# Shift and scale of four channel tiles as product and sum along a channel's weights on VectorE, the other tiles in pairs, and x normalized in front

## The chip, the cores and the metric

The kernel runs on one core of one Trainium2 chip. The metric is the device time in microseconds of one execution. A core has five engines with an instruction stream each: TensorE (PE, whose weight loads are listed as PEld), VectorE (DVE), ScalarE (ACT), GpSimd (POOL) and SyncE (SP, which here issues the loads). Each engine works through its own stream in order, and semaphores hold an instruction until its data or its buffer is ready.

## What is computed

One layer of a hybrid backbone over 256 latent tokens and 256 context tokens, with d = 2048 channels, all in float32. The stage that the change touches computes the modulated, normalized input and the first columns of its projection:

```
sc = jax.nn.silu(c)
scc = jax.nn.silu(c_ctx)
shift, scale, gate = jnp.split(sc @ w_ada[l] + b_ada[l], 3, axis=-1)
shift_c, scale_c, gate_c = jnp.split(scc @ w_ada[l] + b_ada[l], 3, axis=-1)
hc = _rmsnorm(ctx, g_pre[l]) * (1.0 + scale_c) + shift_c
zc = hc @ w_in[l][:, :XBC_W + DT_W]
...
hx = _rmsnorm(x, g_pre[l]) * (1.0 + scale[:, None]) + shift[:, None]
zx = hx @ w_in[l]
```

Behind it stand a convolution and silu, a bidirectional state-space scan over both streams, a gated MLP group over the latent tokens, and the output projection. The change leaves all of that as it is.

## The kernel before

**Layout.** Channels lie on the 128 partitions, in 16 tiles (kt = 0 to 15); xT holds both streams, 512 tokens to a tile (context in columns 0 to 255, latent in 256 to 511). Every float32 product runs as three matmuls, on a rounded part and a rest of each factor: hhi and hlo are the two parts of the modulated input, hi_st and lo_st those of the weights. The helper mm3 (L138 to L140) issues the three.

**The first stage.** SP loads xT in four transfers of 1 MB, then wada (shift and scale weights, 32 transfers of 1 MB, two for each channel tile) and wst (the first 960 columns of the input projection, a transfer of 0.48 MB for each tile). The squares of x (L264 on DVE for odd tiles, L266 on ACT for even ones) are summed on PE into pss, and a few small steps turn that into rb, 1/rms for every token on all partitions. While that runs, `warm` (L256) issues matmuls on ones, whose result nobody reads.

**Shift and scale.** `ada_mm(ci)` multiplies chunk ci of wada, one transfer, with silu(c) and silu(c_ctx) on PE into psada (L215). The tiles come in units: tile 0, tile 1, then pairs; a pair has four chunks. `ada_fin(u)` transposes psada into adat on DVE (L222), and ACT makes ha = g (1 + scale) and hb = shift from it, two small activations for each tile (L224, L226).

**The modulated input.** `make_h(kt)` multiplies a tile of xT by ha and rb (two DVE instructions for the two streams, L307), adds hb and rounds to hhi (two ACT instructions, L310), and takes the rest to hlo (two on DVE, L312). `split_st(kt)` splits wst: a cast on ACT (L299) and two differences on DVE (L300, L301).

**The products of the stage.** For each tile PE adds two matmuls to psdt (L362, L363) and three each to seven column blocks psx0 to psx6. In the order of a row these are the steps ("m", -1) for psdt and ("m", 0) to ("m", 6). The function `row_steps(kt)` lists what stands in row kt: m (those steps), a (`ada_mm`), f (`ada_fin`), h (`make_h`) and s (`split_st`) of the next tile. In the last row `z` copies two finished psx to the segments zq (L357), and `dt_tok` copies psdt and brings its columns to tokens with eight matmul passes pstok (L320) against the matrix fold, which a reduce on DVE (L165) has made from the identity at the start.

**What sets the order.** PE, DVE, ACT and POOL are under a manual schedule: instructions stand in the order in which the code issues them. SP's loads stand in the order of the code too, and each waits for its buffer: six raw buffers for wada, three for wst.

Of the kernel before, what the change touches and what calls it, by code (L numbers as in the profile page):

```python
# [41 lines left out]
def tile_hybrid_ssd_mlp(  # L42
# [121 lines left out]
    A = yseg(7)[:, 320:384]  # L164
    nc.vector.tensor_reduce(fold, ident.rearrange("p (g m) -> p m g", g=2), axis=mybir.AxisListType.X, op=ALU.add)  # L165
# [12 lines left out]
    sc2 = stp.tile([P, KT, 2], F32, name="sc2")  # L178
    nc.sync.dma_start(sc2, ccols)
# [9 lines left out]

    def ada_place(ci):  # L190

        if ci < 4:
            return ci // 2, 64, 8 * (ci % 2), 8
        return ci // 4 + 1, 128, 4 * (ci % 4), 4

    def ada_load(*cs):
# [8 lines left out]
    def ada_mm(ci):  # L205
        u, n, k0, nk = ada_place(ci)
        if k0 == 0:
            ada_ps[u] = spt([P, 512], f"psada{u}")
        ps = ada_ps[u]
        raw = ada_raw.pop(ci)  # L210
        for kk in range(nk):
            k = k0 + kk
            for g in range(4):
                o = (kk * 4 + g) * n
                nc.tensor.matmul(ps[32 * g : 32 * g + 32, 0:n], lhsT=sc[:, k, :], rhs=raw[:, o : o + n],  # L215
                                 start=k == 0, stop=k == KT - 1)

    def ada_fin(u):
# [3 lines left out]
        nc.vector.transpose(tr[:, 0:n], ps[:, 0:n])  # L222
        for q, kt in enumerate(UNITS[u]):
            nc.scalar.activation(ha[:, kt, :], tr[:, 64 * q : 64 * q + 2], AF.Identity, bias=bsc1[:, kt : kt + 1],  # L224
                                 scale=pc[:, C_GPRE + kt : C_GPRE + kt + 1])
            nc.scalar.activation(hb[:, kt, :], tr[:, 64 * q + 32 : 64 * q + 34], AF.Identity,  # L226
                                 bias=pc[:, C_BADA + kt : C_BADA + kt + 1])
# [33 lines left out]
    for k in range(KT):
        sq = yseg((1, 2, 3, 6, 0)[k % 5])
        if k % 2:
            nc.vector.tensor_tensor(sq, xT[:, k, :], xT[:, k, :], op=ALU.mult)  # L264
# [3 lines left out]
        nc.tensor.matmul(pss[32 * g : 32 * g + 32, :], lhsT=ones[:, 0:32], rhs=sq, start=k < 4, stop=k >= KT - 4)
# [26 lines left out]
    def split_st(kt):  # L295
        raw = wraw[kt]
        hi = wp["spl"].tile([P, WST + 64], F32R, tag="hi", name=f"hi_st{kt}")
        lo = wp["spl"].tile([P, WST - 64], F32R, tag="lo", name=f"lo_st{kt}")
        nc.scalar.copy(hi[:, 64:], raw)  # L299
        nc.vector.tensor_tensor(hi[:, 0:64], raw[:, 0:64], hi[:, 64:P].bitcast(F32), op=ALU.subtract)  # L300
        nc.vector.tensor_tensor(lo, raw[:, 64:], hi[:, P:].bitcast(F32), op=ALU.subtract)  # L301
        return hi, lo

    def make_h(kt):
        sl = (slice(256, 512), slice(0, 256))
        for v, s in enumerate(sl):
            nc.vector.scalar_tensor_tensor(xT[:, kt, s], xT[:, kt, s], ha[:, kt, v : v + 1], rb[:, s],  # L307
                                           op0=ALU.mult, op1=ALU.mult)
        for v, s in enumerate(sl):
            nc.scalar.activation(hhi[kt][:, s], xT[:, kt, s], AF.Identity, bias=hb[:, kt, v : v + 1])  # L310
        for v, s in enumerate(sl):
            nc.vector.scalar_tensor_tensor(hlo[kt][:, s], xT[:, kt, s], hb[:, kt, v : v + 1],  # L312
                                           hhi[kt][:, s].bitcast(F32), op0=ALU.add, op1=ALU.subtract)


    def dt_tok():
        nc.scalar.copy(zdt, psdt)
        ps = spt([P, 4, 64], "pstok")
        for t in range(4):
            nc.tensor.matmul(ps[:, slot[t], :], lhsT=zdt[:, t * P : (t + 1) * P], rhs=fold, start=True, stop=True)  # L320
        nc.vector.tensor_tensor(zt.rearrange("p (t h) -> p t h", t=4), ps, bc(dtc, 1, 4), op=ALU.add)
# [3 lines left out]
    def row_steps(kt):  # L325


        m = [("m", i) for i in range(-1, NST)]
# [16 lines left out]
        return nxt[1:] + a + f + nxt[:1] + m

    def step(kt, what, i):
        if what == "a":
# [5 lines left out]
        elif what == "s":  # L354
            sp0[i] = split_st(i)
# [13 lines left out]
    sp0[0] = split_st(0)  # L369
    ada_fin(0)  # L370
    make_h(0)
    for kt in range(KT):
# [848 lines left out]
```

## Time and profile before

| | us |
|---|---|
| three runs | 998.97, 999.53, 1000.25 |
| median | 999.53 |
| the profiled execution, its own time | 999.99 |
| its span in the trace | 998.3 |
| first psdt matmul (tile 0) starts | 23.21 |
| last tile's psdt matmul starts | 128.63 |
| first matmul of the next stage starts | 134.16 |

Times within the span count from its start. "Tile" in the rows that follow is a channel tile. The page gives busy time for each engine; a window gives the same for a stretch of the span; the chain follows back from the last instruction to what released it; the groups sum instructions of one line and shape and say what ended the idle time ahead of them (behind the second bar, after the arrow); the timeline lists instructions with start, duration and, in brackets, the idle time ahead with its releaser. In the rows of a single source line the three numbers behind the colon are the shortest, median and longest duration in ns, and "x64" behind a matmul counts passes, of which a float32 matmul whose parts aren't rounded has several.

### The profile page before, as it was taken

The numbers are of one execution on the slowest core, as the hardware profiler recorded it, in microseconds if no ns is written. First come the engines' busy times: TensorE is split into PE (matmuls) and PEld (weight loads), VectorE is DVE, ScalarE is ACT, GpSimd is POOL, SyncE is SP. The second block draws the span as 40 slices with busy tenths as digits, with TensorE's granted clock in tenths as the row PEclk, the third lists the DMA queues.
The fourth block names the chain that finished last, engine by engine and source line by source line (L and its number), as shares of the span: only waits on it lengthen the run. The fifth ranks groups of instructions, "written<-read, shape, count | busy, mean of one in ns | idle before, by whom it ended". The sixth has DMA issues, their size and how long they took to land.

```text
span 998.3 us, 14183 instructions
## 1 busy us (share of the span) xinstructions
PE 977.1 (98%) x5636; PEld 791.3 (79%) x5636; DVE 629.9 (63%) x944; ACT 493.0 (49%) x759; POOL 113.7 (11%) x162
## 2 busy tenths in 40 slices
PE   7999999999999999999999999999999999999996
PEld 3788888778687878787888888877888888888885
DVE  4344478877977665666667766666565564445636
ACT  4233347666656545544445343455565564346522
POOL 0000003423443222224000000000000000000000
PEclk9999999999999999999999999999999999999998
DMA  9999744333224323235878778674555545556722
GB/s 380 419 417 419 293 175 143 111 127 127 85 85 165 103 112 133 79 127 195 311 283 297 275 258 319 252 274 172 185 173 191 188 169 209 175 207 231 274 85 84
DMA packets 31554, 207.28 MB, mean 208 GB/s; under 512 B 4080, under 2 KB 4208, under 8 KB 7808
## 3 DMA queue, kind: packets, MB, share of 16 engines
q1 hardware_dynamic: 28656, 192.52, 51.5%
q0 software_dynamic: 2112, 12.65, 3.6%
q10 hardware_dynamic: 720, 1.20, 0.3%
q8 instruction: 44, 0.72, 0.3%
q14 instruction: 22, 0.18, 0.1%
HBM read 204.20 MB, written 2.16 MB: 207 GB/s over the span
## 4 chain that ended last, share of the span: by engine, by line
PE 69%; issue 11%; DMA 9%; DVE 8%; POOL 1%; ACT 1%; SPq 0%; DVEq 0%; POOLq 0%; ACTq 0%
PE psx L138 9%; PE psx L140 9%; PE psx L139 9%; PE pa L1026 5%; PE pa L1028 5%; PE pa L1027 5%; DMA gate<-in_wada_dram 5%; PE pm L1073 3%; PE pm L1075 3%; PE pm L1074 3%; PE psada L215 3%; DVE xbc L495 2%; PE pq L1075 2%; PE pq L1073 2%; PE pq L1074 2%
## 5 line engine op out<-in xcount | busy, mean ns | idle before, releaser
L82 DVE TENSOR_TENSOR lo_w<-w,hi_w 128x1024 fp32r<-128x1024 f32 x173 | 210.5, 1224 | 144.3 <-ACT hi_w L81 144.3
L81 ACT CAST hi_w<-w 128x1024 fp32r<-128x1024 f32 x173 | 182.1, 1053 | 202.5 <-PE pa L1028 130.5
L1026 PE MATMUL pa<-hi_w,hhi 128*128 128x512 f32 x512 | 202.5, 395 | 0.0
L1028 PE MATMUL pa<-hi_w,hlo 128*128 128x512 f32 x512 | 199.5, 390 | 0.0
L1027 PE MATMUL pa<-lo_w,hhi 128*128 128x512 f32 x512 | 199.4, 389 | 0.0
L138 PE MATMUL psx<-hhi,hi_w 128*128 128x512 f32 (+1 forms) x400 | 153.5, 384 | 1.3 <-DVE xbc L495 1.3
L140 PE MATMUL psx<-hhi,lo_w 128*128 128x512 f32 (+1 forms) x400 | 146.0, 365 | 0.0
L139 PE MATMUL psx<-hlo,hi_w 128*128 128x512 f32 (+1 forms) x400 | 145.7, 364 | 0.0
L1026 PEld LDWEIGHTS pa<-hi_w,hhi 128*128 128x128 f32 x512 | 96.2, 188 | 20.7 <-issue 1.6
L1028 PEld LDWEIGHTS pa<-hi_w,hlo 128*128 128x128 f32 x512 | 96.1, 188 | 20.2
L1027 PEld LDWEIGHTS pa<-lo_w,hhi 128*128 128x128 f32 x512 | 96.2, 188 | 19.4 <-issue 0.2
L495 DVE SCALAR_TENSOR_TENSOR xbc<-psx,pc,xbc 128x248 f32<-128x248 f32 (+1 forms) x204 | 83.6, 473 | 36.6 <-ACT xbc L479 35.6
L420 DVE TENSOR_TENSOR lo_w<-w,hi_w 128x1024 fp32r<-128x1024 f32 x61 | 78.1, 1287 | 25.0 <-ACT hi_w L414 25.0
L138 PEld LDWEIGHTS psx<-hhi,hi_w 128*128 128x128 f32 x400 | 75.5, 189 | 15.0 <-issue 3.1
L140 PEld LDWEIGHTS psx<-hhi,lo_w 128*128 128x128 f32 x400 | 75.4, 189 | 12.6
L139 PEld LDWEIGHTS psx<-hlo,hi_w 128*128 128x128 f32 x400 | 75.6, 189 | 12.1 <-issue 1.7
L414 ACT CAST hi_w<-w 128x1024 fp32r<-128x1024 f32 x61 | 63.4, 1044 | 26.4 <-PE pa L1028 13.3
L884 DVE SCALAR_TENSOR_TENSOR junk<-gate,cb 128x2048 bf16<-128x2048 f32 x16 | 36.6, 2290 | 24.6 <-DMA gate<-in_wada_dram 24.6
L1073 PE MATMUL pm<-hi_w,hhi 128*128 128x512 f32 x128 | 50.0, 390 | 0.0
L1074 PE MATMUL pm<-lo_w,hhi 128*128 128x512 f32 x128 | 49.9, 390 | 0.0
L1075 PE MATMUL pm<-hi_w,hlo 128*128 128x512 f32 x128 | 49.7, 389 | 0.0
L138 PE MATMUL psx<-hhi,hi_st 128*128 128x512 f32 (+1 forms) x112 | 41.3, 369 | 0.0
(219 smaller groups left out, 1333.7 us busy)
## 6 DMA issues: line engine op xcount, KB each, us to landing
w<-in_wlat_dram SPq DMA_DIRECT2D x64, 1024.0 KB, 4.8
ada<-in_wada_dram SPq DMA_DIRECT2D x32, 1024.0 KB, 14.6
w<-in_wout_dram SPq DMA_DIRECT2D x32, 1024.0 KB, 4.8
w<-in_wxbc_dram SPq DMA_DIRECT2D x25, 1024.0 KB, 4.8
gate<-in_wada_dram SPq DMA_DIRECT2D x16, 1024.0 KB, 5.7
R<-acs POOLq DMA_DIRECT2D x8, 1024.0 KB, 4.9
wst<-in_wst_dram SPq DMA_DIRECT2D x16, 480.0 KB, 14.8
xT<-in_xch_dram SPq DMA_DIRECT2D x4, 1024.0 KB, 8.0
```

The lines of the kernel that those rows point to most:

```text
L81: nc.scalar.copy(hi, raw)
L82: nc.vector.tensor_tensor(lo, raw, hi.bitcast(F32), op=ALU.subtract)
L138: nc.tensor.matmul(ps, lhsT=whi, rhs=hhi[k][:, s], start=start, stop=False)
L139: nc.tensor.matmul(ps, lhsT=whi, rhs=hlo[k][:, s], start=False, stop=False)
L140: nc.tensor.matmul(ps, lhsT=wlo, rhs=hhi[k][:, s], start=False, stop=stop)
L495: nc.vector.scalar_tensor_tensor(ao, zi, cw[:, k : k + 1], ao, op0=ALU.mult, op1=ALU.add)
L1026: nc.tensor.matmul(pa[tk], lhsT=hhi[k][:, t], rhs=whi[:, w], start=k == 0, stop=False)
L1027: nc.tensor.matmul(pa[tk], lhsT=hhi[k][:, t], rhs=wlo[:, w], start=False, stop=False)
L1028: nc.tensor.matmul(pa[tk], lhsT=hlo[k][:, t], rhs=whi[:, w], start=False, stop=k == KT - 1)
L1073: nc.tensor.matmul(p, lhsT=yh[:, t], rhs=whi[:, w], start=j == 0, stop=False)
L1074: nc.tensor.matmul(p, lhsT=yh[:, t], rhs=wlo[:, w], start=False, stop=False)
L1075: nc.tensor.matmul(p, lhsT=yl[:, t], rhs=whi[:, w], start=False, stop=hf == 0 and j == 15)
```

## The change

Four of the 16 channel tiles, 7, 10, 13 and 15 (VTILES), get shift and scale on DVE. Their weights lie transposed in wada, one channel on each partition, and `ada_v` multiplies the 2048 weights of a channel with silu(c) and sums along them in one instruction (four for a tile: scale and shift, each with c and with c_ctx). For that silu(c) and silu(c_ctx) must stand on all partitions; `c_rows` makes them in the first stage with eight diagonals on DVE and eight matmuls against ones (psr), and `c_keep` copies them to y on ACT. They stand where `warm(1)` stood in the loop over the squares. The other tiles form the units (0), (1), (2,3), (4,5), (6,8), (9,11), (12,14).

A table of strings, WITH, now sets each row's order: `p4` is four of the row's own steps m, `a4.1` a chunk of unit 4, `f`, `h` and `s` as before, `v10.0.1` one sum of tile 10 (0 for scale, 1 for c_ctx), `e10` its ha and hb, `n` the normalizing of tiles 4 to 15. A string LOADS sets the order of the transfers, `room` and `give` issue each as soon as a buffer is free. There are five raw buffers at first, as the sixth holds the squares (sq4), and six from rb on. The bytes moved are the same.

1/rms is multiplied into xT in front (`norm`, one DVE instruction for each tile). `make_h` then has no products on DVE: ACT forms x ha + hb, for tiles 0 to 3 straight into hhi (and DVE a second time in full precision), from tile 4 on into xT itself, followed by a cast into hhi; hlo is one DVE instruction over 512 columns. The split of wst runs two tiles ahead. The reduce for fold moves into `dt_tok`, as y's segments hold the rows of silu(c) until then; A gets a buffer of its own.

```diff
+UNITS = ((0,), (1,), (2, 3), (4, 5), (6, 8), (9, 11), (12, 14))
+VTILES = (7, 10, 13, 15)
+LOADS = "u0.0 w0 u0.1 u1.0 u1.1 w1 w2 u2.0 u2.1 u2.2 u2.3 w3 w4 v7.0 u3.0 u3.1 u3.2 u3.3 w5 v7.1 w6 u4.0 u4.1 u4.2 u4.3 " \
+        "w7 w8 w9 v10.0 v10.1 u5.0 u5.1 u5.2 u5.3 w10 w11 w12 v13.0 v13.1 u6.0 u6.1 u6.2 u6.3 w13 w14 v15.0 w15 v15.1"
+WITH = (
+    "p2 a1.0 a1.1 f1 h1 n p4 a2.0 p2 a2.1",
+    "p2 a2.2 p2 a2.3 f2 h2 h3 s3 p4",
+    "s4 v7.0.0 v7.0.1 p6 a3.0 p2 a3.1",
+    "p2 a3.2 p2 a3.3 f3 h4 s5 h5 p4",
+    "v7.1.0 s6 v7.1.1 e7 h7 p6 a4.0 p2 a4.1",
+    "p2 a4.2 p2 a4.3 f4 h6 s7 h8 p4",
+    "s8 v10.0.0 p8",
+    "s9 v10.0.1 v10.1.0 p4 a5.0 p2 a5.1 p2 a5.2",
+    "v10.1.1 e10 h10 p3 a5.3 f5 h9 s10 h11 p5",
+    "s11 v13.0.0 p8",
+    "s12 v13.0.1 v13.1.0 p3 a6.0 p2 a6.1 p2 a6.2 p1",
+    "v13.1.1 e13 h13 p1 a6.3 f6 h12 s13 h14 p7",
+    "s14 v15.0.0 v15.0.1 p8",
+    "s15 v15.1.0 v15.1.1 e15 h15 p8",
+    "p8",
+    "",
+)
...
+    def ada_v(kt, c, v):
+        raw = ada_raw[f"v{kt}.{c}"]
+        nc.vector.scalar_tensor_tensor(junk, raw, 1.0, y[:, v, :], op0=ALU.mult, op1=ALU.mult,
+                                       accum_out=vsum[:, kt, c, v : v + 1])
...
+    def c_rows(*bs):
+        for b in bs:
+            v, k = b // 4, 4 * (b % 4)
+            dg = junk4[:, (b % 2) * 512 : (b % 2 + 1) * 512].rearrange("p (k m) -> p k m", k=4)
+            nc.vector.tensor_tensor(dg, bc(ident, 1, 4), bc(sc[:, k : k + 4, v], 2, P), op=ALU.mult)
+            cbp[b] = acp.tile([P, 512], F32, tag="acc", name=f"psr{b}")
+            nc.tensor.matmul(cbp[b], lhsT=ones, rhs=dg, start=True, stop=True)
+
+    def c_keep(*bs):
+        for b in bs:
+            nc.scalar.copy(y[:, b // 4, (b % 4) * 512 : (b % 4 + 1) * 512], cbp.pop(b))
...
     warm(2)
+    c_rows(0, 1)
...
         if g == 3:
-            warm(1)
+            b = k // 4 * 2
+            c_keep(b, b + 1)
+            if b < 6:
+                c_rows(b + 2, b + 3)
...
+    def norm(*ks):
+        for k in ks:
+            nc.vector.tensor_tensor(xT[:, k, :], xT[:, k, :], rb, op=ALU.mult)
...
     def make_h(kt):
...
-        for v, s in enumerate(sl):
-            nc.vector.scalar_tensor_tensor(xT[:, kt, s], xT[:, kt, s], ha[:, kt, v : v + 1], rb[:, s],
-                                           op0=ALU.mult, op1=ALU.mult)
-        for v, s in enumerate(sl):
-            nc.scalar.activation(hhi[kt][:, s], xT[:, kt, s], AF.Identity, bias=hb[:, kt, v : v + 1])
-        for v, s in enumerate(sl):
-            nc.vector.scalar_tensor_tensor(hlo[kt][:, s], xT[:, kt, s], hb[:, kt, v : v + 1],
-                                           hhi[kt][:, s].bitcast(F32), op0=ALU.add, op1=ALU.subtract)
+        x = xT[:, kt, :]
+        if kt < 4:
+            for v, s in enumerate(sl):
+                nc.scalar.activation(hhi[kt][:, s], x[:, s], AF.Identity, bias=hb[:, kt, v : v + 1],
+                                     scale=ha[:, kt, v : v + 1])
+            full = ss4
+            for v, s in enumerate(sl):
+                nc.vector.tensor_scalar(full[:, s], x[:, s], ha[:, kt, v : v + 1], hb[:, kt, v : v + 1],
+                                        op0=ALU.mult, op1=ALU.add)
+        else:
+            full = x
+            for v, s in enumerate(sl):
+                nc.scalar.activation(x[:, s], x[:, s], AF.Identity, bias=hb[:, kt, v : v + 1], scale=ha[:, kt, v : v + 1])
+            nc.scalar.copy(hhi[kt], x)
+        nc.vector.tensor_tensor(hlo[kt], full, hhi[kt].bitcast(F32), op=ALU.subtract)
...
     def dt_tok():
+        nc.vector.tensor_reduce(fold, ident.rearrange("p (g m) -> p m g", g=2), axis=mybir.AxisListType.X, op=ALU.add)
         nc.scalar.copy(zdt, psdt)
```

Where the order of instructions matters below, here it is at three places. Names carry the number of a buffer behind the last underscore, "x2" is two alike in a row.

PE before, at the end of the loop over the squares (psw is a filler matmul, psb the step towards 1/rms, psada0 the products of unit 0), up to the first product of tile 0:

```order
L268 MATMUL pss_193<-y_68,ones_95 32x512 x4
L256 MATMUL psw_190<-ones_95 128x512
L276 MATMUL psb_231<-y_68,sel_163 128x16
L215 MATMUL psada0_238<-ada_0_172,sc_159 32x64 x32
L215 MATMUL psada0_238<-ada_1_176,sc_159 32x64 x32
L256 MATMUL psw_190<-ones_95 128x512 x2
L362 MATMUL psdt_305<-hhi0_117,hi_st0_312 128x512
```

PE now, from the last two psr on:

```order
L314 MATMUL psr6_246<-junk4_161,ones_95 128x512
L314 MATMUL psr7_249<-junk4_161,ones_95 128x512
L331 MATMUL pss_202<-sq4_166,ones_95 32x512 x4
L341 MATMUL psb_262<-junk4_161,sel_163 128x16
L256 MATMUL psada0_271<-ada_u0_0_175,sc_158 32x64 x32
L256 MATMUL psada0_271<-ada_u0_1_179,sc_158 32x64 x32
L303 MATMUL psw_193<-ones_95 128x512 x2
L441 MATMUL psdt_342<-hhi0_117,hi_st0_349 128x512
```

Two matmuls that wait for diagonals stand where one filler stood, ahead of the squares of the next four tiles.

ACT before, where the tiles 6 and 7 get their shift and scale from unit 4 (adat4):

```order
L224 ACTIVATE ha_111<-adat4_817,bsc1_112,pc_87 128x2
L226 ACTIVATE hb_110<-adat4_817,pc_87 128x2
L224 ACTIVATE ha_111<-adat4_817,bsc1_112,pc_87 128x2
L226 ACTIVATE hb_110<-adat4_817,pc_87 128x2
L310 ACTIVATE hhi6_123<-xT_156,hb_110 128x256 x2
L299 CAST hi_st7_858<-wst7_775 128x960
```

ACT now at the same place; tile 7 comes from DVE's sums (vsum), tiles 6 and 8 from unit 4:

```order
L272 ACTIVATE ha_111<-vsum_167,bsc1_112,pc_87 128x2
L274 ACTIVATE hb_110<-vsum_167,pc_87 128x2
L390 ACTIVATE xT_155<-xT_155,hb_110,ha_111 128x256 x2
L391 CAST hhi7_124<-xT_155 128x512
L272 ACTIVATE ha_111<-adat4_893,bsc1_112,pc_87 128x2
L274 ACTIVATE hb_110<-adat4_893,pc_87 128x2
L272 ACTIVATE ha_111<-adat4_893,bsc1_112,pc_87 128x2
L274 ACTIVATE hb_110<-adat4_893,pc_87 128x2
L390 ACTIVATE xT_155<-xT_155,hb_110,ha_111 128x256 x2
L391 CAST hhi6_123<-xT_155 128x512
```

Between hb and a tile's hhi stand two activations over 256 tokens and a cast over 512, where two activations into hhi stood.

DVE before, at the last tiles of the stage:

```order
L222 STREAM_TRANSPOSE adat8_1417<-psada8_1316 128x128
L307 SCALAR_TENSOR_TENSOR xT_156<-xT_156,ha_111,y_68 128x256 x2
L312 SCALAR_TENSOR_TENSOR hlo14_147<-xT_156,hb_110,hhi14_131 128x256 x2
L300 TENSOR_TENSOR hi_st15_1452<-wst15_1378,hi_st15_1452 128x64
L301 TENSOR_TENSOR lo_st15_1453<-wst15_1378,hi_st15_1452 128x896
L307 SCALAR_TENSOR_TENSOR xT_156<-xT_156,ha_111,y_68 128x256 x2
L312 SCALAR_TENSOR_TENSOR hlo15_148<-xT_156,hb_110,hhi15_132 128x256 x2
L357 COPY y_68<-psx4_310 128x512
```

DVE now, from hlo of tile 12 on (junk4 takes the products of the sums, which nobody reads):

```order
L392 TENSOR_TENSOR hlo12_145<-xT_155,hhi12_129 128x512
L366 TENSOR_TENSOR hi_st13_1268<-wst13_1096,hi_st13_1268 128x64
L367 TENSOR_TENSOR lo_st13_1269<-wst13_1096,hi_st13_1268 128x896
L392 TENSOR_TENSOR hlo14_147<-xT_155,hhi14_131 128x512
L366 TENSOR_TENSOR hi_st14_1298<-wst14_1122,hi_st14_1298 128x64
L367 TENSOR_TENSOR lo_st14_1299<-wst14_1122,hi_st14_1298 128x896
L266 SCALAR_TENSOR_TENSOR junk4_161,vsum_167<-ada_v15_0_1154,y_68 128x2048 x2
L366 TENSOR_TENSOR hi_st15_1328<-wst15_1156,hi_st15_1328 128x64
L367 TENSOR_TENSOR lo_st15_1329<-wst15_1156,hi_st15_1328 128x896
L266 SCALAR_TENSOR_TENSOR junk4_161,vsum_167<-ada_v15_1_1184,y_68 128x2048 x2
L392 TENSOR_TENSOR hlo15_148<-xT_155,hhi15_132 128x512
```

The four sums of tile 15 stand behind hlo14 and the splits of tiles 13 and 14, and tile 15's own hlo stands behind them.

More of the change, by code (lines that the diff above doesn't have):

```diff
@@ L354, in step @@
         elif what == "s":
-            sp0[i] = split_st(i)
+            split_st(i)
+        elif what == "v":
+            ada_v(i, *r)
+        elif what == "e":
+            ada_vfin(i)
+        elif what == "n":
+            norm(*range(4, KT))
         elif what == "z":
```

137 lines of the change are left out of this document (76 added, 61 removed).

## The prediction

> **What bounds the kernel now.** I read the page's busy shares and its chain first, then the windows of the first stage (0 to 134 us), because the diff touches nothing behind it, then that stage's chain, its groups and single instructions.
>
> ```profile
> PE 977.1 (98%) x5636; PEld 791.3 (79%) x5636; DVE 629.9 (63%) x944; ACT 493.0 (49%) x759; POOL 113.7 (11%) x162
> ...
> 5.00:20.00 15.00, 11.60 (x119) 4.36 (x123) 8.83 (x17) 6.78 (x12) 0.00 (x0) 1.00 1.01 425
> 20.00:50.00 30.00, 27.56 (x459) 20.29 (x451) 11.78 (x26) 8.54 (x19) 0.00 (x0) 1.00 1.02 420
> 50.00:80.00 30.00, 30.00 (x417) 24.71 (x417) 14.36 (x30) 11.21 (x25) 0.00 (x0) 1.00 1.01 415
> ...
> 110.00:134.00 24.00, 24.00 (x233) 20.34 (x233) 11.99 (x25) 10.41 (x19) 0.00 (x0) 1.00 0.55 218
> DMA packets 8222, 46.08 MB, mean 397 GB/s; under 512 B 1424, under 2 KB 1552, under 8 KB 3600
> ```
>
> A window's row gives its length, then busy time of PE, PEld, DVE, ACT and POOL, the granted clock, the DMA share and GB/s. In 50 to 80 and in 110 to 134 us PE is busy all the time while DVE has about half the window free: TensorE bounds the stage. The transfers run at their full share until about 115 us, but nothing in 50 to 134 us waits for them, and the change moves the same bytes. So the stage gets shorter by what PE loses, if DVE and ACT can take the work without making PE wait. This is what I add up, against the profiled execution (999.99 us, span 998.3), which lies 0.46 above the median shown (999.53). The part behind 134 us I take as shifted as a whole.
>
> **What leaves PE.**
>
> ```profile
> 65.30 0.43 PE psdt L362
> ...
> 68.06 0.12 PE psx L138
> ...
> 70.15 1.89 PE psada L215 x64
> 72.03 0.43 PE psdt L362
> ...
> 76.88 1.88 PE psada L215 x64
> 78.77 0.43 PE psdt L362
> ...
> 124.02 0.23 PE psdt L362
> 128.63 0.23 PE psdt L362
> ```
>
> In the chain (start, duration, line) two product chunks of a pair stand as x64 with 1.88 us, so a chunk is 0.94. Four tiles lose two chunks each: 8 x 0.94 = **-7.5**. A tile with two chunks takes 72.03 - 65.30 = 6.73, one without 128.63 - 124.02 = 4.61: the 2.12 between is 1.88 and 0.24 for the switch between the two kinds of matmul. Before there are 18 groups of chunks in a row, the new table cuts them into 21: 3 x 0.25 = **+0.75**.
>
> **The waits of before.**
>
> ```profile
> L215 PE MATMUL psada<-ada,sc 128*32 128x128 f32 x896 | 28.0, 274 | 0.3 <-DMA ada<-in_wada_dram 0.3
> L215 PE MATMUL psada<-ada,sc 128*32 128x64 f32 x256 | 4.4, 220 | 1.6 <-DMA ada<-in_wada_dram 1.5
> L362 PE MATMUL psdt<-hhi,hi_st 128*128 128x512 f32 x16 | 7.7, 483 | 2.0 <-DVE hi_st L300 1.6 <-ACT hhi L310 0.4
> ```
>
> These groups (17 to 134 us; after the second bar the idle time ahead) hold 3.9 us of PE's waits, 0.4 of them ahead of the first psdt. The 1.6 for hi_st goes, as the split runs two tiles ahead, and most of the DMA's goes, as the units start later. I leave 0.5: **-3.0**. At worst the DMA's 1.9 stay.
>
> **The start.**
>
> ```profile
> 13.60 1.13 PE L256 MATMUL psw<-ones 128*128 128x512 f32 x2
> 14.65 1.46 PE L268 MATMUL pss<-y,ones 128*32 128x512 f32 x8
> 23.21 0.51 PE L362 MATMUL psdt<-hhi,hi_st 128*128 128x512 f32 x1 [0.39 <-ACT hhi L310]
> L264 DVE TENSOR_TENSOR y<-xT x8: 684/690/693, 6.3 to 14.3; 128x512 f32<-128x512 f32 x8
> L307 DVE SCALAR_TENSOR_TENSOR xT<-xT,ha,y 128x256 f32<-128x256 f32 x32 | 14.1, 481 | 4.1 <-ACT ha L224 4.1
> L317 ACT COPY y<-psdt x1: 588/588/588, 129.1 to 129.1; 128x512 f32<-128x512 f32 x1
> ```
>
> A round of four squares costs PE 1.46 and one filler matmul of about 0.85 (13.60 to 14.65, less its hand-off), which is 2.3; xT comes at the same pace (the squares on DVE are those of every second tile: 14 tiles from 6.3 to 14.3, so 2.3 for four). Now three rounds carry two psr matmuls instead of the filler, 1.46 + 1.7 = 3.15, and DVE has two diagonals (0.69, as the square) beside two squares, 2.8. Three rounds x 0.85 put 1/rms 2.55 later. The first of make_h's products (0.48) leaves the chain from adat to hhi; norm(0), 0.69, runs while PE has unit 0's chunks. 2.55 - 0.48 is 2.1, and 0.1 for hand-offs: the first psdt starts at 25.4 instead of 23.2, **+2.2**. If the psr matmuls hide in PE's own waits of these rounds it is 0; if the copies (0.588) stand in line as well, 2.55 + 2 x 0.588 = 3.7.
>
> **The new waits.** The work that DVE gets, and the chain that now ends in hhi:
>
> ```profile
> L884 DVE SCALAR_TENSOR_TENSOR junk<-gate,cb x16: 2284/2292/2294, 478.5 to 650.6; 128x2048 bf16<-128x2048 f32 x16
> L884 DVE DVE_READ_ACCUMULATOR junk<-gate,cb x16: 80/83/84, 480.7 to 652.8; 128x1 f32 x16
> L301 DVE TENSOR_TENSOR lo_st<-wst,hi_st x16: 1079/1084/1087, 19.2 to 122.6; 128x896 fp32r<-128x896 f32 x16
> L300 DVE TENSOR_TENSOR hi_st<-wst,hi_st 128x64 fp32r<-128x64 f32 x16 | 3.6, 223 | 23.7 <-ACT hi_st L299 23.7
> L431 DVE TENSOR_TENSOR hlo<-w,hhi x16: 684/685/694, 912.5 to 950.7; 128x512 fp32r<-128x512 f32 x16
> 119.23 0.32 DVE L222 STREAM_TRANSPOSE adat<-psada 128x128 f32<-128x128 f32 x1 [2.94 <-PE psada L215]
> 119.59 0.39 ACT L224 ACTIVATE ha<-adat,bsc,pc 128x2 f32<-128x2 f32 x1 [4.55 <-DVE adat L222]
> 120.35 0.28 ACT L226 ACTIVATE hb<-adat,pc 128x2 f32<-128x2 f32 x1
> 120.59 0.91 ACT L310 ACTIVATE hhi<-xT,hb 128x256 fp32r<-128x256 f32 x2
> L310 ACT ACTIVATE hhi<-xT,hb 128x256 fp32r<-128x256 f32 x32 | 14.6, 502 | 13.1 <-DVE xT L307 13.1
> L479 ACT ACTIVATE xbc<-y,pc x3: 604/817/817, 229.1 to 261.5; 128x512 f32<-128x512 f32 x2, 128x256 f32<-128x256 f32 x1
> L430 ACT CAST hhi<-w x16: 612/618/625, 911.2 to 949.3; 128x512 fp32r<-128x512 f32 x16
> ```
>
> A shift and scale on DVE is four such sums, 2.29 + 0.08 = 2.37 each. A split of wst is 0.22 + 1.08 = 1.3 on DVE, hlo in one piece 0.69. Behind a unit's last chunk stand: adat 0.32, four small activations 1.04 (119.59 to 120.59), two halves with scale and bias, 0.604 by L479's smaller form but overlapping as L310's do (two in 0.91), so 1.1, and a cast of 0.62; with hand-offs 3.3. PE has four groups of psx beside it: 0.35 + 0.69 + 0.69 + 0.35 = 2.1 (the chain above, from 68.06 to 70.15), and 0.2 in the pipeline. So it waits 1.0 to 1.1. Then hlo (0.69) comes while PE has one matmul of 0.23, so 0.5 more. By place in the table:
>
> - Pair 2,3: its hhi is still in the short form, but twelve norms (12 x 0.69 = 8.3) stand ahead of its adat on DVE: 0.7 + 0.5 = 1.2.
> - Pairs 4,5 and 6,8: 1.1 + 0.5 each, 3.2.
> - Pair 9,11: from tile 6's start DVE has hlo6, s7, hlo8, s8, a sum, s9 and three sums: 2 x 0.69 + 3 x 1.3 + 4 x 2.37, with hand-offs 15.4. Only then come tile 10's hb 0.28, halves 1.1, cast 0.62, hlo10 0.69, and behind these the pair's adat 0.32, small ones 1.04, halves and cast 1.7: 21.5 with 0.3 of hand-offs. PE has three tiles (13.8), four chunks with switches (4.8) and its earlier half microsecond: 19.3. Wait 2.2 + 0.5.
> - Pair 12,14, behind tile 13's sums: the same, 2.7.
> - Tile 15: from tile 12's start two hlo, two splits, two sums, a split and two sums: 1.4 + 3.9 + 9.5, with hand-offs 15.4, then hb, halves, cast 2.1. PE has three tiles without any chunks, 13.8 + 0.5: wait 3.2 + 0.5 = 3.7.
>
> Together 1.2 + 3.2 + 2.7 + 2.7 + 3.7 = **+13.5**. Below: nothing, if all hides. Above: a sum by four times L431's 0.685 is 2.74; 0.37 more on four sums makes three waits longer by 1.5 each, 4.5 more. I take 2.37, since L884 is the same operation with an accumulator at the same size. [...]
>
> **The end of the stage.**
>
> ```profile
> 129.83 1.37 DVE L357 COPY y<-psx 128x512 f32<-128x512 f32 x2 [4.27 <-PE psx L140]
> 130.31 1.00 PE L320 MATMUL pstok<-y 128*128 128x64 f32 x8
> 7.48 0.28 DVE L165 TENSOR_REDUCE y<-ident 128x64 f32<-128x128 f32 x1
> ```
>
> The reduce that makes fold moves from 7.48 into dt_tok. There it stands on DVE behind the two zq copies, and pstok, which started at 130.31 while they ran, waits until 129.83 + 1.37 + 0.28 and a hand-off: **+1.25**. Nothing hides it; PE's other work stands behind pstok.
>
> **Sum:** -7.5 + 0.75 - 3.0 + 2.2 + 13.5 + 1.25 = +7.2, so 999.99 + 7.2 = **1007.2**. The norms, hb and ha of the DVE tiles and the earlier small DMAs I cost at nothing beyond this: DVE's and ACT's free halves hide them.
>
> **Rivals.**
>
> A, the other side: *the new waits hide*. It needs sums of at most 1.7 us, so that DVE is ahead at pairs 9,11 and 12,14 and at tile 15, and a chain behind adat of under 2.3, so that four groups cover it. Then 13.5 goes: 999.99 - 6.3 = 993.7. It is faster by 0.2% from the point where the new waits come to under 4.3. For it: PE waits leave DVE time to run ahead, for the sums need nothing of PE. Against: 2.29 is measured sixteen times with a spread of 10 ns.
>
> D: *half of them hide*, since DVE keeps the lead that one stall gives it and the three long waits are one: 1007.2 - 6.6 = 1000.6.
>
> B: *the sums cost more*, 2.6 to 2.74, and DVE sets the pace from tile 6 to 15: 3 x (0.23 to 0.37) x 4 = 2.8 to 4.5 more, 1010 to 1011.7; I put it at 1010. For it: two f32 reads from SBUF, and the DMAs write beside it.
>
> C: *the clock falls in the tail's wait.*
>
> ```profile
> 1.12 3.78 PE L256 MATMUL psw<-ones 128*128 128x512 f32 x4 [1.12 <-DVE ones L107]
> 20.84 1.99 PE L256 MATMUL psw<-ones 128*128 128x512 f32 x4
> ```
>
> The same four passes took 3.78 at the start and 1.99 later. If a stall of 3.2 brings the slow pace back for as long, 1.8 more: 1009.0. Against: PE is idle for 3.4 of the 15 us from 5 to 20, and the granted clock stands at 1.00 in that window and in those behind it. [...]
>
> **How the numbers follow.** Forecast 0.62, A 0.09, D 0.12, B 0.11, C 0.06. A measurement of this kernel tells about 0.2%, 2 us. Forecast, B and C lie slower; A faster; D (998 to 1003) is 0.07 within and 0.05 slower. So faster 0.09, same 0.07, slower 0.84. The range leaves out A and half of D at the bottom and half of B at the top: 1001.0 to 1011.0.
>
> **What would show it.** The first psdt at 25.4 instead of 23.2; idle time ahead of psdt put down to hhi and hlo, about 13 us in all and longest ahead of tiles 9, 12 and 15; the sums at 2.29 + 0.08; psada at 24 pair chunks of 0.94; pstok released by fold; the stage's end near 141. It is wrong if DVE shows gaps ahead of the sums (then their data or buffers are late), if PE is still busy throughout from 50 us on, or if what lies behind the stage changes its length.

## The result and the profile after

| | before | changed |
|---|---|---|
| median, us | 999.89 (998.97 to 1001.30) | 1010.74 (1009.72 to 1012.82) |
| ratio, 95% interval | | 1.0113 (1.0097 to 1.0130) |
| profiled execution, its span | 999.99, 998.3 | 1010.50, 1008.4 |
| first psdt matmul | 23.21 | 24.59 |
| end of the stage (first matmul of the next, by the timeline) | 134.00 | 145.11 |
| from there to the end | 864.29 | 863.31 |

The changed kernel is slower by 1.1%. All of it arises in the stage, which ends 11.1 us later; what lies behind it is 1.0 shorter (a wait of 0.7 for the tile vt, at 657 us of the profile of before, isn't there).

The page's busy shares and the windows of the changed kernel (columns as before):

```profile
PE 978.6 (97%) x5388; PEld 785.8 (78%) x5388; DVE 665.3 (66%) x959; ACT 507.4 (50%) x779; POOL 113.6 (11%) x162
...
5.00:20.00 15.00, 13.93 (x122) 5.00 (x126) 11.10 (x20) 10.72 (x20) 0.00 (x0) 1.00 1.01 424
20.00:50.00 30.00, 24.74 (x393) 17.80 (x382) 21.79 (x43) 10.36 (x21) 0.00 (x0) 0.94 0.96 392
50.00:80.00 30.00, 27.77 (x341) 20.62 (x341) 16.80 (x21) 13.21 (x28) 0.00 (x0) 1.00 1.01 416
...
110.00:134.00 24.00, 22.37 (x162) 17.82 (x160) 18.18 (x21) 9.45 (x18) 0.00 (x0) 1.00 0.56 219
134.00:146.00 12.00, 8.45 (x35) 6.49 (x36) 5.83 (x11) 7.68 (x12) 0.00 (x0) 0.86 0.30 126
```

Where PE was busy for 30.00 of 30 us it is now busy for 27.77, and two windows have a granted clock below 1. The waits view names what PE waited for (total, times, longest), the timeline the places:

```profile
PE psdt L441 <- ACT hhi L391: 6.7, 5, 2.4
PE psada L256 <- issue: 2.8, 1, 2.8
PE psdt L441 <- ACT hhi L381: 1.9, 2, 1.7
...
PE psdt L442 <- DVE hlo L392: 1.6, 7, 0.2
...
PE pstok L400 <- DVE y L396: 1.1, 1, 1.1
```

```profile
31.18 0.64 PE L256 MATMUL psada<-ada_u,sc 128*32 128x128 f32 x16
34.63 1.08 PE L256 MATMUL psada<-ada_u,sc 128*32 128x128 f32 x16 [2.81 <-issue]
...
77.82 0.49 PE L441 MATMUL psdt<-hhi,hi_st 128*128 128x512 f32 x1 [0.88 <-ACT hhi L391]
78.54 0.50 PE L442 MATMUL psdt<-hlo,hi_st 128*128 128x512 f32 x1 [0.23 <-DVE hlo L392]
...
98.52 0.50 PE L441 MATMUL psdt<-hhi,hi_st 128*128 128x512 f32 x1 [1.24 <-ACT hhi L391]
...
136.25 0.50 PE L441 MATMUL psdt<-hhi,hi_st 128*128 128x512 f32 x1 [2.45 <-ACT hhi L391]
136.98 0.79 PE L442 MATMUL psdt<-hlo,hi_st 128*128 128x512 f32 x1 [0.22 <-DVE hlo L392]
137.57 0.63 PE L164 MATMUL psx<-hhi,hi_st 128*128 128x512 f32 x1
138.00 0.63 PE L165 MATMUL psx<-hlo,hi_st 128*128 128x512 f32 x1
```

Three things are to be seen. The waits for hhi and hlo stand where the new chain ends. In the middle of one chunk (the same line, 16 passes and 16 passes) PE stands still for 2.81 us and waits for nothing that the profile shows. And behind the longest wait matmuls that start each 0.23 us elsewhere start each 0.43: half the clock, granted at 0.50 from 136.67 to 140.09 us.

A wait costs more than its idle time, since a matmul's modelled end (0.40) lies 0.17 behind the next one's start: for hhi idle plus 0.17; for hlo 0.72 (77.82 to 78.54) instead of 0.24, so 0.48. In what follows "the chain" is the way from a unit's last chunk to hhi (adat, ha and hb, halves, cast), "cover" is the work that PE has beside it, and "refill" is that extra of 0.17 or 0.48.

### The profile page after: what moved, and what is told of

Its sections match the earlier page's. It is cut to its first block, busy times and chain, and to the rows that moved or that the text cites. A ratio compares the mean times of both kernels' runs of the same rounds, so it can differ in the third digit from the quotient of the medians.

```text
span 1008.4 us, 13732 instructions
## 1 busy us (share of the span) xinstructions
PE 978.6 (97%) x5388; PEld 785.8 (78%) x5388; DVE 665.3 (66%) x959; ACT 507.4 (50%) x779; POOL 113.6 (11%) x162
## 4 chain that ended last, share of the span: by engine, by line
PE 84%; DVE 8%; ACT 3%; issue 3%; POOL 1%; DMA 0%; DVEq 0%; ACTq 0%; POOLq 0%
PE pa L1105 11%; PE pa L1107 11%; PE pa L1106 11%; PE psx L164 8%; PE psx L166 7%; PE psx L165 7%; PE pm L1152 3%; PE pm L1153 3%; PE pm L1154 3%; DVE junk L266 2%; DVE xbc L574 2%; PE pq L1152 2%; PE pq L1153 2%; PE pq L1154 2%; PE psada L256 1%
## 5 line engine op out<-in xcount | busy, mean ns | idle before, releaser
L1106 PEld LDWEIGHTS pa<-lo_w,hhi 128*128 128x128 f32 x512 | 96.2, 188 | 19.3 <-issue 0.2
L164 PEld LDWEIGHTS psx<-hhi,hi_w 128*128 128x128 f32 x400 | 75.5, 189 | 14.9 <-issue 3.1
## 6 DMA issues: line engine op xcount, KB each, us to landing
ada_u<-in_wada_dram SPq DMA_DIRECT2D x24, 1024.0 KB, 13.5
```

Source lines behind the costliest of these rows:

```text
L164: nc.tensor.matmul(ps, lhsT=whi, rhs=hhi[k][:, s], start=start, stop=False)
L1106: nc.tensor.matmul(pa[tk], lhsT=hhi[k][:, t], rhs=wlo[:, w], start=False, stop=False)
```

## The experiments

All were run with the profile and against the kernel before, whose median lay between 999.23 and 999.42 in them. "Stage" is the stage's end in the profile; the last column counts the stretches of 3.41 us at half clock within the stage. Both are of one profiled execution; in e2 that was its fastest (1005.62), 4.8 us below the median.

| kernel | median, us | ratio (95%) | stage | half clock |
|---|---|---|---|---|
| changed | 1010.74 | 1.0113 (1.0097 to 1.0130) | 145.11 | 2 |
| e1 small loads late | 1007.02 | 1.0076 (1.0064 to 1.0088) | 141.81 | 1 |
| e2 two sums of tile 15 earlier | 1010.43 | 1.0099 (1.0083 to 1.0116) | 140.29 | 1 |
| e3 fold early | 1009.73 | 1.0108 (1.0093 to 1.0122) | 143.53 | 2 |
| e4 e1, norms spread | 1006.73 | 1.0071 (1.0059 to 1.0083) | 141.42 | 1 |
| e5 e1, no sums on DVE | 1014.43 | 1.0144 (1.0126 to 1.0163) | 149.25 | 0 |
| e6 changed, filler ahead of tile 15 | 1008.39 | 1.0088 (1.0073 to 1.0103) | 143.43 | 1 |
| e7 e1, fold early, hlo's matmuls later | 1004.31 | 1.0044 (1.0030 to 1.0058) | 138.98 | 1 |
| e8 e7, more cover, tile 15 on PE | 998.87 | 0.9991 (0.9981 to 1.0001) | 133.18 | 0 |
| e9 e7, more cover at three pairs | 1002.80 | 1.0033 (1.0020 to 1.0045) | 136.39 | 0 |
| e10 e7, short chain | 999.61 | 1.0003 (0.9995 to 1.0012) | 134.62 | 1 |
| e11 e9 and e10, tile 15 on PE | 998.50 | 0.9994 (0.9985 to 1.0003) | 133.31 | 0 |

**The stall in the chunk (e1).** The question is whether three small loads, which now move at 29 to 33 us, hold up the transfer of PE's instructions and so make the stall.

```diff
         if kt == 5:
+            for q in (dtc, A, dsk):
+                nc.vector.memset(q[:, 0:1], 0.0)
             nc.sync.dma_start(dtc, dtp[0:1].partition_broadcast(P))
```

> The three small loads (dtc, A, dsk) are held back to row 5, nothing else changes. [...] Then the 2.8 and the half clock at 34.3 go. But the twelve norms end at 41.3 in any case and adat of pair 2,3 stands behind them, so its hhi can't come before 43.9 (now 46.35): the time falls by 2.4, to about 1008.3, and by no more than 4.5. Rival: the stall comes from the dense run of chunks (unit 1's two and unit 2's first close together); then it stays at 2.8 and the time at 1010.7.

In the changed kernel SP issued the three loads at 16 to 20 us and they moved at 28.7 to 32.8; before the change it issued them at 57.7 to 59.5. In e1 DVE writes a column of each buffer in row 5, and the loads, which wait for that, move at 78.9 to 81.8. Windows of one us, of the changed kernel and of e1 (columns as before):

```profile
29.00:30.00 1.00, 1.00 (x7) 0.82 (x6) 1.00 (x3) 0.25 (x1) 0.00 (x0) 1.00 0.33 71
...
32.00:33.00 1.00, 0.00 (x0) 0.00 (x0) 0.61 (x2) 0.40 (x1) 0.00 (x0) 1.00 0.93 375
...
35.00:36.00 1.00, 1.00 (x17) 0.60 (x10) 1.00 (x2) 0.00 (x0) 0.00 (x0) 0.50 1.05 442
```

```profile
29.00:30.00 1.00, 1.00 (x6) 0.81 (x5) 1.00 (x3) 0.53 (x1) 0.00 (x0) 1.00 1.06 442
...
32.00:33.00 1.00, 0.48 (x16) 0.38 (x16) 0.61 (x3) 0.68 (x2) 0.00 (x0) 1.00 1.02 426
...
35.00:36.00 1.00, 1.00 (x19) 0.71 (x12) 1.00 (x3) 0.00 (x0) 0.00 (x0) 1.00 1.00 413
```

With the small loads late the DMA share stays at 1 and the stall is 0.7 instead of 2.8; the half clock behind it is gone. The place in e1's timeline:

```profile
32.52 0.65 PE L256 MATMUL psada<-ada_u,sc 128*32 128x128 f32 x16 [0.72 <-issue]
```

Transfers of instructions have queues of their own in the trace; q8 moves 16 KB at a time, 42 times in the changed kernel, once for some 250 of PE's instructions. The DMA view of 28 to 32 us shows none of them in the changed kernel and one in e1:

```profile
q1 hardware_dynamic: 501, 0.87, 59.0%
```

```profile
q1 hardware_dynamic: 233, 1.65, 100.0%
q8 instruction: 1, 0.02, 1.7%
```

In the changed kernel that transfer starts at 32.14 and takes 0.94, and PE goes on at 34.63, 2.5 us behind its start. e1 has one between 28 and 32 us, and PE goes on at 32.52; before the change one started at 28.14, and PE's waits list no stall. The other profiles fit this. With the small loads at 29 to 33 us the stall is 2.8 (changed), 2.3 (e3), 2.1 (e6) and 0.7 (e2, where PE, at a clock of 0.50 in 26 to 28 us, reached the place 0.9 later: at 32.73 instead of 31.82). With them held back and the same start it is 0.7 (e1, e4), 0.4 (e8) and 0.3 (e9), and the waits of e7, e10 and e11 list none. So the small loads make the stall long. That PE waits there for its instructions is the author's reading of these times, since the view names no releaser, and when such a transfer is asked for, no trace shows. The rival, a dense run of chunks by itself, doesn't make the stall long: the run is in e1 too. Why three loads of 0.08 MB in all leave the DMA engines idle for about 1.7 us, when at 67 to 69 us of the profile of before the same three left the share at 1, is not settled. The time fell by 3.7 rather than 2.4; 0.9 of the 1.3 between is that tile 2 started at 42.97, not 43.9.

**The norms (e4).**

```diff
-    "p2 a1.0 a1.1 f1 h1 n p4 a2.0 p2 a2.1",
-    "p2 a2.2 p2 a2.3 f2 h2 h3 s3 p4",
+    "p2 a1.0 a1.1 f1 h1 n4.6 p4 a2.0 p2 a2.1",
+    "p2 a2.2 p2 a2.3 f2 n6.8 h2 h3 s3 p4",
...
+    "p2 a3.2 p2 a3.3 f3 n8.12 h4 s5 h5 p4",
+    "p2 a4.2 p2 a4.3 f4 n12.16 h6 s7 h8 p4",
```

> The small loads late as in the first run, and the twelve norms spread: two in row 0, two behind adat of pair 2,3, four each behind adat of pairs 4,5 and 6,8. Theory: the norms were what came late next; now hhi of tile 2 follows its last chunk by about 2.6 instead of waiting for DVE, and the time falls by the whole 4.5 (stall 2.8, half clock 1.7), to about 1006.2. Rival: four norms behind an adat push the next hlo back and PE waits 1 us longer at pairs 4,5 and 6,8, or the transfers set the pace of rows 0 to 2: 1008 to 1009, like the first run.

Tiles 8 to 15 are multiplied by other numbers than 1/rms here, since the sums' products overwrite rb; instructions and sizes are the same. It gains 0.3 over e1, less than the executions of either spread (1005.0 to 1007.65 and 1005.8 to 1008.6); the theories of the two lay 2.1 apart (1008.3 and 1006.2). In e1 PE's wait ahead of tile 2 is 0.30 already: the norms are not what comes late.

**The tail (e2) and the clock (e6).**

```diff
-    "v13.1.1 e13 h13 p1 a6.3 f6 h12 s13 h14 p7",
-    "s14 v15.0.0 v15.0.1 p8",
+    "v13.1.1 e13 h13 p1 a6.3 f6 v15.0.0 v15.0.1 h12 s13 h14 p7",
+    "s14 p8",
```

> Two of tile 15's four sums move on DVE from behind hlo14 to the place behind adat of pair 12,14, where DVE stands idle for about 5 us. Theory: DVE's backlog of sums sets tile 15; 4.7 us less of it there takes away the wait of 2.6 ahead of tile 15, the 0.6 for its hlo and the half clock from 136.7 on (1.7): 1010.7 - 4.9 = 1005.8. Rival: the sums meet late transfers (tile 15's first half landed at 113.6) and push hlo12 back, so tile 12 waits longer by what tile 15 saves: 1009 to 1011, with the half clock at tile 12.

The median (1010.43) is the rival's. The profiled execution (1005.62) has the theory's time, but partly for another reason: its stall at 33 us was 0.7 instead of 2.8. In that profile tile 15 no longer waits, but the two sums hold up hlo12, and tile 12 waits for it (1.91 instead of 0.23):

```profile
116.88 0.50 PE L441 MATMUL psdt<-hhi,hi_st 128*128 128x512 f32 x1 [1.23 <-ACT hhi L391]
119.30 0.49 PE L442 MATMUL psdt<-hlo,hi_st 128*128 128x512 f32 x1 [1.91 <-DVE hlo L392]
```

Its executions spread from 1005.62 to 1011.32, and with them the mean clock: 0.996 at 1005.62, 0.992 at 1011.32. One stretch at half clock takes 0.0017 from the mean (3.41 x 0.5 of 1005), so two more of them, at about 1.5 us each (below), may be some 3 of these 5.7 us. That is an estimate and not shown: the slower executions have no trace, and the mean clock of the kernel before varies from 0.995 to 0.998 with no such change in its time. e6 tests the clock by itself:

```diff
+        elif what == "w":
+            wt = spt([P, 512], "psw2")
+            for _ in range(i):
+                nc.tensor.matmul(wt, lhsT=ones, rhs=ones[:, 0:1].to_broadcast([P, 512]), start=True, stop=True)
...
-    "p8",
+    "p8 w3",
```

> The changed kernel with three filler matmuls on ones ahead of tile 15's first product, where PE stands idle for 2.45 us; nothing reads them. Theory: the half clock from 136.7 on follows a stretch of 3.4 us in which PE was idle for most of the time; with the fillers it is busy, the clock stays at 1.00 and the eight matmuls behind it take 0.23 instead of 0.43 each: 1010.7 - 1.7 = 1009.0, the stage's end 1.7 earlier against the start of tile 15's psdt. Rival: the granted clock falls for another reason (load, time); then tile 15 starts up to 0.3 later and the time is 1011.

The windows ahead of and behind tile 15's first product, of the changed kernel and of e6:

```profile
133.00:137.00 4.00, 1.33 (x7) 0.72 (x6) 1.79 (x3) 2.00 (x4) 0.00 (x0) 0.96 1.01 424
137.00:140.00 3.00, 3.00 (x7) 2.13 (x7) 0.69 (x1) 2.16 (x4) 0.00 (x0) 0.50 0.19 79
```

```profile
133.00:137.00 4.00, 3.77 (x12) 1.79 (x12) 1.52 (x3) 2.00 (x4) 0.00 (x0) 1.00 1.01 428
137.00:140.00 3.00, 1.93 (x10) 1.30 (x10) 1.58 (x3) 2.72 (x4) 0.00 (x0) 1.00 0.08 33
```

With PE busy on nothing useful the clock stays at 1.00; from tile 15's psdt to the stage's end it takes 7.44 instead of 8.86, so this stretch of half clock cost 1.4 us. In the changed kernel the wait (133.80 to 136.25) lies inside one stretch of the clock (133.26 to 136.67); where the stretches lie in e6, its windows don't show. The median falls by 2.35 (1.7 forecast); part of that isn't the filler's, since the stall in this profile was 2.1 instead of 2.8.

**The fold (e3).** The reduce moves to the end of the row before the last.

```diff
-        nc.vector.tensor_reduce(fold, ident.rearrange("p (g m) -> p m g", g=2), axis=mybir.AxisListType.X, op=ALU.add)
         nc.scalar.copy(zdt, psdt)
...
-    "p8",
+    "p8 d",
```

> The reduce for fold stands behind tile 15's hlo on DVE instead of behind the two copies in the last row. Theory: pstok's wait of 1.07 (1.25 with the pipeline) goes and nothing else: 1009.5, the stage ends 1.2 us earlier. Rival: the wait is for the copy of psdt on ACT or for the two copies on DVE, and pstok starts as late as before: 1010.7.

pstok's wait is gone from the list of waits, and the median is 1009.73. By the time alone 1.0 can't be told from 0 here, since this profile has another stall (2.3) and 6.8 us at half clock. The tail tells it: from tile 15's psdt to the stage's end e3 takes 6.11 at full clock, e6, at full clock with pstok's wait, 7.44. The 1.3 between is the wait of 1.07 and its refill, 1.24, within 0.1.

**The sums (e5).** UNITS holds seven pairs, VTILES nothing, and `warm(1)` stands in the loop over the squares again.

```diff
-UNITS = ((0,), (1,), (2, 3), (4, 5), (6, 8), (9, 11), (12, 14))
-VTILES = (7, 10, 13, 15)
+UNITS = ((0,), (1,), (2, 3), (4, 5), (6, 7), (8, 9), (10, 11), (12, 13), (14, 15))
+VTILES = ()
...
+    "s6 p6 a4.0 p2 a4.1",
+    "p2 a4.2 p2 a4.3 f4 h6 s7 h7 p4",
```

> The first run (small loads late) with all 16 tiles' shift and scale on PE again: tiles 2 to 15 in pairs, no sums on DVE, no rows of silu(c), one filler matmul in each round of squares as before the change; the new make_h, the norms in front and the fold in the last row stay. Theory: what costs is the longer way from a chunk to hhi (two halves into xT, cast, hlo in one piece), which pairs pay wherever they stand, and not the sums: eight chunks come back (7.5), seven pairs wait about 1.6 each (11.5, as now), the start comes 1.4 earlier, and the wait ahead of tile 15 goes with its half clock (1.7): 1007.0 + 7.5 - 0.75 - 1.4 - 1.7 = 1010.7. Rival: DVE's backlog of sums is what costs; without the sums the waits fall to before's 3.5 and the time to about 1002.

It is 7.4 slower than e1, though its first psdt starts 1.8 earlier (22.99) and no stretch runs at half clock. PE's waits in e5 (the first 1.5 of the transfers' 2.9 lies ahead of the first psdt):

```profile
PE psdt L437 <- ACT hhi L387: 5.3, 6, 0.9
PE psada L256 <- DMA ada_u<-in_wada_dram: 2.9, 2, 1.5
```

Without a single sum each of the six pairs from 4,5 on still waits 0.9 for hhi, as 4,5 and 6,8 do in the changed kernel. So what costs at every pair is the longer chain from chunk to hhi, sums or not; DVE's sums add 0.3 to 0.4 at tiles 9 and 12 and the wait at tile 15. The size was off (1010.7 expected) mainly because of the table: it cuts the chunks into 29 groups where the changed kernel's has 21 and before's had 18, so eight switches are added, 2.2 us at 0.28 each, where the sum took off 0.75. A wait of 1.4 for a transfer (at 29.8) comes on top. So the 7.4 isn't the worth of the sums alone: they do pay here, by about 5 us at most, as 2.2 are the table's.

**The chain: hlo later (e7), more cover (e9), a shorter chain (e10).** e7 is e1 and e3 with hlo's matmuls later in the row; e9 and e10 are each e7 with one thing more.

```diff
+            nc.tensor.matmul(psx[j], lhsT=wh, rhs=hhi[kt], start=kt == 0, stop=False)
+            nc.tensor.matmul(psx[j], lhsT=wl, rhs=hhi[kt], start=False, stop=False)
             nc.tensor.matmul(psdt, lhsT=whi[:, 0:P], rhs=hlo[kt], start=False, stop=last)
+            nc.tensor.matmul(psx[j], lhsT=wh, rhs=hlo[kt], start=False, stop=last)
```

> The first run, with fold's reduce behind tile 15's hlo as in the third, and with the two matmuls on hlo (psdt's and that of the row's first psx) put behind the three on hhi. Theory: the second wait of every unit, for hlo, 0.23 us in the trace and 0.5 to 0.6 with the pipeline that runs dry, is covered by two matmuls of 0.23: seven times 0.5 less the part that hhi's wait takes over behind the long chains, 1.8, and 1.2 from fold: 1007.0 - 3.0 = 1004.0. Rival: the waits for hhi grow by what those for hlo lose, since the same chain of activations stands behind both: 1005.8.

```diff
-    "p2 a3.2 p2 a3.3 f3 h4 s5 h5 p4",
+    "p1 a3.2 p1 a3.3 f3 h4 s5 h5 p6",
```

> The run with hlo's matmuls put back (1004.3), and in rows 1, 3 and 5 the last two chunks of the pair one group of psx earlier each, so that six groups (3.5 us) stand beside the chain to hhi instead of four (2.1). Theory: at pairs 4,5 and 6,8 the wait is the chain less its cover, so 1.0 to 1.4 us go at each; the transfers take back 0.8 at unit 4, and the sums' places (tiles 9, 12, 15) wait as before: 1004.3 - 1.8 = 1002.5. Rival: the chain's length isn't what ends late, DVE's or ACT's other work is; then hhi comes as late as before and the time stays at 1004.

```diff
     def make_h(kt):
...
-        if kt < 4:
+        if True:
```

> The run with hlo's matmuls put back (1004.3), with make_h for all tiles in the form that tiles 0 to 3 have: ACT writes hhi at once, DVE forms the full sum a second time (two instructions of 0.41 each) and then hlo. Theory: the cast of 0.62 leaves every chain, twice where a pair stands behind a single tile's ha and hb (tiles 9 and 12), and once at 15: the waits at tiles 4, 6, 9, 12 and 15 fall by 0.6, 0.6, 1.3, 1.3 and 0.7, together 4.5: 1004.3 - 4.5 = 999.8; the half clock ahead of tile 15 may go as well (1.7 more). Rival: DVE is the bound by then, and its 0.8 us a tile, ten us in all, push the sums back: 1004 or later.

1004.31, 1002.80 and 999.61 against 1004.0, 1002.5 and 999.8. The waits for hhi of the three kernels, and in the last two those for transfers, in this order:

```profile
PE psdt L445 <- ACT hhi L391: 8.1, 5, 2.9
PE psdt L445 <- ACT hhi L381: 2.3, 2, 1.3
```

```profile
PE psdt L445 <- ACT hhi L391: 6.0, 3, 2.9
PE psada L256 <- DMA ada_u<-in_wada_dram: 3.4, 4, 1.2
PE psdt L445 <- ACT hhi L381: 1.6, 1, 1.6
```

```profile
PE psdt L445 <- ACT hhi L381: 4.8, 5, 2.0
PE psada L256 <- DMA ada_u<-in_wada_dram: 2.3, 4, 1.0
```

e7 has no wait for hlo left. With six groups beside the chain (e9) the waits at pairs 4,5 and 6,8 are gone, three at tiles 9, 12 and 15 remain; without the cast (e10) hhi's waits fall from 10.4 to 4.8. In both, waits for the transfers take part of the place. e9 and e10 show the cause from two sides: the wait for hhi goes with more cover and with a shorter chain, the sums unchanged.

**Together (e8, e11).** Tile 15 goes back to PE as a unit of its own, unit 5's and 6's adat ahead of the single tiles' (e8); e11 has the short chain and the changed kernel's order of the sums.

```diff
-VTILES = (7, 10, 13, 15)
+VTILES = (7, 10, 13)
...
-    "v10.1.1 e10 h10 p3 a5.3 f5 h9 s10 h11 p5",
+    "p2 a5.3 v10.1.1 f5 h9 e10 v13.0.0 h10 s10 h11 p6",
...
-    "s15 v15.1.0 v15.1.1 e15 h15 p8",
+    "s15 p2 a7.0 p1 a7.1 f7 h15 p5",
```

> The run before, with tile 15 back on PE as a unit of its own (two chunks of 0.96, so PE has 1.9 more), each pair's last two chunks one group of psx earlier (six groups stand beside the chain to hhi instead of four), unit 5's and 6's adat ahead of the single tile's ha and hb, and tile 13's first sum behind unit 5's adat. Theory: the waits are gone but for 1.0 at tile 2 and pieces under 1, no 3.4 us are idle enough for the half clock, and the stage ends at 131.0 to 132.0 against 134.0 before the change: 996.5 to 998, faster than before (999.3) by 0.15 to 0.3%. Rival: the transfers, which now land as PE needs them (0.9 late at unit 4), set the pace, or PE's fetch of instructions stalls as before: 999 to 1001.

> The fastest version so far (998.9), with the short form of make_h for all tiles, and the sums in the order of the changed kernel's table. Theory: in that version PE waits for the transfers of wada (3.4 us in five places), which run without a gap, so a shorter chain gains nothing: 998.9, the stage's end at 133 again. Rival: the chain still sets a part; then 997 to 998.

PE's waits in e8, then in e11:

```profile
PE psada L256 <- DMA ada_u<-in_wada_dram: 3.4, 5, 1.2
...
PE psdt L445 <- ACT hhi L381: 1.7, 1, 1.7
```

```profile
PE psada L256 <- DMA ada_u<-in_wada_dram: 5.4, 6, 1.4
...
PE psdt L445 <- ACT hhi L381: 1.2, 1, 1.2
```

Only the first tile waits for hhi any more. A shorter chain (e11) turned into longer waits for transfers, 5.4 instead of 3.4, and the stage ended at 133.31 instead of 133.18: the transfers set the pace, which was e8's rival (999 to 1001; e8's 998.87 lies just below it and above the theory's 998). Both medians lie below before's by 0.6 and 0.7 us, and both intervals still hold 1: as fast as before, not shown to be faster.

## Why the prediction was wrong in size, step by step

The direction held, and the time lay inside the range near its top: forecast +7.2 on the profiled execution, measured +10.5.

- **Sums.** Taken at 2.29 + 0.08, and so they are, in the groups of the changed kernel (17 to 148 us; busy us, mean ns). Rival B fell.

```profile
L266 DVE SCALAR_TENSOR_TENSOR junk<-ada_v,y 128x2048 bf16<-128x2048 f32 x16 | 36.6, 2288 | 0.2
...
L266 DVE DVE_READ_ACCUMULATOR junk<-ada_v,y 128x1 f32 x16 | 1.3, 82 | 0.0
```

- **Products and switches,** -7.5 and +0.75. The chunks left and the 21 groups are as counted, but a switch is dearer: tile 10 takes 8.27 with three single chunks and no wait, 8.27 - 4.61 - 2.82 leaves 0.84 for three switches, 0.28 each instead of 0.25. That is 0.6 more over 21. e5 against e1 is 7.4 as well, but by chance: its start, clock, waits and switches differ too.
- **Waits of before,** -3.0, was misread. Of the transfers' waits in its groups 1.45 lies ahead of the first psdt (23.21), and so in the start, which is a term of its own. The timeline of before:

```profile
19.80 1.10 PE L215 MATMUL psada<-ada,sc 128*32 128x64 f32 x64 [1.45 <-DMA ada<-in_wada_dram]
...
32.41 1.08 PE L215 MATMUL psada<-ada,sc 128*32 128x128 f32 x32 [0.34 <-DMA ada<-in_wada_dram]
...
42.33 0.50 PE L362 MATMUL psdt<-hhi,hi_st 128*128 128x512 f32 x1 [1.58 <-DVE hi_st L300]
```

Behind the first psdt stood only 0.34 and 1.58, 2.3 with refill. None of them is left: -2.3.

- **Start,** +2.2: measured 1.4, since a round took 2.9, not 3.15 (pss starts at 7.95, 10.86, 13.77 and 16.68).
- **New waits,** +13.5: their places were all right, their sizes too large. At tiles 2, 4, 6, 9, 12, 15 forecast 1.2, 1.6, 1.6, 2.7, 2.7, 3.7; measured (idle + 0.17 + 0.48) 0.9, 1.5, 1.5, 1.9, 1.9, 3.1. That is 10.8, and 0.5 for tile 0's hlo; A and D, in which all or half would hide, fell. At tile 9 DVE's 15.4 from hlo6 to the end of the sums were 14.9 (77.80 to 92.73) and the 6.1 behind them 5.8 (to 98.52). PE's 19.3 there add up to 19.1 by their own parts, so the forecast of 2.2 should have read 2.4.
- **Fold,** +1.25: idle 1.07 and 0.17, right.
- **The step that failed** is the sentence behind the sum: "the earlier small DMAs I cost at nothing beyond this". They brought the stall of 2.8 at 31.8, which e1 cut to 0.7, and the half clock behind it. That is some 4.3 us where the sum has nothing; with the loads late the kernel is 3.7 faster.
- **Rival C,** the clock in the tail's wait, had 0.06 and came true, as e6 shows, at a somewhat lower price (1.8 forecast, 1.4 measured). It struck twice, in the stall as well: from tile 0's psdt to tile 1's the changed kernel takes 3.63 more than e1, of which 2.18 is idle time, so that stretch cost 1.45. It stood as a rival and not in the sum, though the forecast itself had a wait of 3.2 there.

The measured terms: -7.5 + 0.75 + 0.6 - 2.3 + 1.4 + 11.3 + 1.25 + 2.8 + 2.9 = +11.2, and the stage ends 11.1 later; the agreement is closer than the terms are known. Behind the stage, taken as shifted as a whole, the time is 1.0 shorter. Against the forecast the stall, the two stretches of half clock, the switches and the waits of before make 7.0 more, the new waits and the start 3.0 less. That the time still fell inside the range is in part luck: errors of both signs.

## What to carry to other kernels

Work taken from the bound engine pays only as far as the chain that replaces it is covered: count what the bound engine still has to do between the moment at which the chain can start and the moment at which it needs the result (here four groups, 2.1 us, left a wait of 0.9, and six, 3.5 us, left none), and move that start before anything else. A wait on PE is priced with what follows from it, the refill (0.17 and 0.48 here) and the half clock, which followed the waits of 2.45 and 2.81 us here (1.4 and 1.45 us) and not e9's of 2.9. Small loads without a buffer to wait for can move ahead in a load queue when buffers are handed out differently (here from 57.7 to 59.5 us to 16 to 20, by issue); look where they land.

## What was not expected of the hardware

In the profile of the changed kernel the granted clock is 0.50 from 34.27 to 37.69 us and from 136.67 to 140.09, 3.41 us each time; between the two it is 1.00 for 98.99 us, 29 times 3.413. In stretches of that length, laid out from the start of its clock record (6.97), PE was idle for 2.55 us of the stretch that ends at 34.27 and for 2.45 of the one that ends at 136.67. The others of the stage have 1.34 or less, and the clock stayed at 1.00 behind them, as it did behind the longest in the stage of before, 1.67 (5.28 to 8.69) and 1.58 (39.41 to 42.82). With the second wait filled, in e6, it stayed at 1.00. The idle time isn't the whole of it: e9 has a wait of 2.9 for hhi and no stretch at half clock in the stage, and e2's clock was 0.50 in 26 to 28 us behind no wait of over 1.4. What decides there was not shown. So a wait of 2 to 3 us cost a stretch of half clock here (1.4 and 1.45 us in the changed kernel) or nothing.

PE's instructions come by DMA as well: q8, of the kind "instruction", started one transfer for some 250 of them. The one at the stall started at 32.14 us; before the change, when the small loads moved later, one started at 28.14. PE went on 2.5 us behind the start at 32.14; the waits view calls the stall, 2.8 us, "issue".
